# Taking the tensor work of the mixing stages off GpSimd: the S5 scan rebuilt for VectorE, the weight splits, rotary products and decays moved, one convolution tap given to ScalarE

## The chip, the cores and the metric

The kernel runs on one core of a Trainium2 chip. The metric is the device time of one execution in microseconds (us). The core has five engines that run their own instruction queues in order: TensorE for matmuls (PE in the profile; PEld are its weight loads), VectorE (DVE), ScalarE (ACT), GpSimd (POOL) and SyncE (SP), which here only starts DMA transfers.

## The reference

The reference is a two-layer trunk over 256 context tokens and 256 latent tokens of width 1024, all in float32. Each layer has a mixing stage and a mixture-of-experts stage (MoE). The mixing stage, cut to what matters:

```
u, z, xbc, dtr, q, k, v, gates = split_cols(h @ w_in)
ya = s5_branch(u, ...)          # complex diagonal SSM: B u, scan, C h, gelu, glu
yb = ssd_branch(z, xbc, dtr...) # 5-tap convolution, silu, chunked scan, gated norm
yc = attention_branch(q, k, v)  # rotary, 128-token window plus context
out = (sum_k sigmoid(gates_k) * (y_k @ w_branch_k)) @ w_out
```

The S5 branch has 32 groups of 16 channels, 64 complex states each, in two directions:

```
bur = einsum('gpk,bngk->bngp', bbr, u);  bui = ...
h_n = a * h_(n-1) + bu_n          # complex, per group and state; reversed for direction 1
y   = einsum('gkp,bngp->bngk', c_re, hr) - einsum('gkp,bngp->bngk', c_im, hi)
```

Layer 0 needs outputs for context and latent tokens (512), layer 1 for the latent tokens alone (256). The MoE stage reads 16 experts' weights, three matrices of 4 MB each.

## The kernel before, in words

**Order.** The program is written layer by layer as `mixing(l)` and `moe(l)`. A list scheduler with a timing model of its own fixes each engine's order when the kernel is built, so instructions of branches that do not depend on each other are interleaved. Tiles wait by semaphores on what was in their space before.

**Weights and splits.** Float32 products of good accuracy are made from split halves. `load_w` (L103) lets SP load a 128x1024 block of weights into `w` (three buffers), ACT copies it rounded into `wh` (L110), and a subtraction makes the rest, `wl` (L113). Two buffers each hold `wh` and `wl`. The subtraction goes to POOL and DVE in turn (`turn`, `wcnt`). `mm3` (L122, L125) then multiplies `wh` by both halves of the activations and `wl` by the high half.

**S5.** `s5_gen` (L585) handles four groups of channels and both directions in one block, eight blocks in a layer, in one set of buffers (four `rb` tiles) and one PSUM bank (`bank("s5")`, one buffer). The names that the steps touch:

- `bc`, `Ub`: the block's parameters and inputs, loaded from the ACT queue (L610, L611). `bb` (L614 to L619) is the discretised B, its real half on DVE and its imaginary half on POOL.
- `gp` (L631 to L633) are the powers that bring eight steps of B together, `cp9` (L637 to L639) those of C. `tmp` holds the second products. Direction 0 is made by DVE (`e = V`), direction 1 by POOL. `ti` are `gp`'s transposes (L642, L643).
- `pk` (L648), `kr` (L650 to L653) and `kd` are the short convolution kernels: `kr` lies in the last 240 columns of `tmp`, goes to DRAM (`kd`, L655) and comes back as `W` (L657).
- `er`, `ei` (L665 to L667) are rotations, the first on DVE, the second on POOL. `px` (L674) are the inputs of the scan; they are rotated (L683 to L688; the two sums on POOL), scanned (L691, eight scans of 64 steps with a decay from `rho`), rotated back (L696 to L699, half on POOL) and written into `hs` (L706 to L709, half on POOL).
- `yp` (L713, L715) is the output, L719 to L722 its gelu, L723 the store to DRAM (`ad`).

**Others on POOL.** The splits of the branch outputs (`splits`, L736; L1122; L1130), one product of the state decay (L898), two of the rotary (L924, L925), the gate product (L958), half of the query splits (L992), the router's weights (L1144, L1145), and preparations that the change leaves alone: memsets, powers in `s5_params` and the one-hot scaling in the MoE stage (L1272).

**Convolution.** `ev_x` (L791) copies a PSUM tile into `xp` (ACT, L800), makes five taps on DVE (L809 and four times L812), a tanh on ACT (L814) and a last product on DVE (L816), for eight tiles in a layer.

**End of a mixing stage.** Three calls of `merge` (L1077) multiply the branch outputs and add them up in `acc` (L1094 to L1097). The first two need the SSD and the attention branch, the third needs S5's outputs through a glu (L1116 to L1122). `w_out` and the router (L1140 to L1200) follow, and then the MoE stage, whose weights stream through the buffers that the mixing stage held.

Of the kernel before, what the change touches and what calls it, by code (L numbers as in the profile page):

```python
# [66 lines left out]
def tile_trunk(ctx: ExitStack, tc: tile.TileContext, a, out, dbg=None, stop=None):  # L67
# [220 lines left out]
    def s5_params(l, sl):  # L288
# [113 lines left out]
        Aa = keep("aa", 640).rearrange("p (q i) -> p q i", i=10)  # L402
        Ab = keep("ab", 640).rearrange("p (q i) -> p q i", i=10)
        G.memset(Aa, 0.0)
        G.memset(Ab, 0.0)
        for dst, lo_, hi_, sgn in ((Aa, PR, PI, 1.0), (Ab, PI, PR, -1.0)):
            for d in range(2):
                for h, (src, sg) in enumerate(((lo_, sgn), (hi_, 1.0))):
# [3 lines left out]
                    ov = ov[:, :, :, 1:10] if d == 0 else ov[:, :, :, 0:9]  # L412
# [50 lines left out]
    def mixing(l, mods):  # L463
# [121 lines left out]
        def s5_gen():  # L585
# [11 lines left out]
            xr, xi = sl(4, 64), sl(4, 64)  # L597
# [3 lines left out]
            kr = tmp.rearrange("p a b -> p (a b)")[:, 784:1024]  # L601
            pq = ti.rearrange("p a b -> p (a b)").rearrange("p (i t c) -> p i t c", i=4, t=4)
            G.memset(bst, 0.0)  # L603
            G.memset(hs, 0.0)
            kd = dram.tile([8, 4, 32, 240], F32, name="kd%d" % l)

            for b in range(8):
# [4 lines left out]
                frb, fib = (sp[n][:, g8, None].to_broadcast([128, 8, 16]) for n in ("fr", "fi"))  # L612
                t0, t1 = (tmp[:, 4 * i].rearrange("p (t k) -> p t k", k=16) for i in range(2))
                V.tensor_tensor(bb[:, 0], bc[:, 0], frb, op=OP.mult)  # L614
                V.tensor_tensor(t0, bc[:, 1], fib, op=OP.mult)
                V.tensor_tensor(bb[:, 0], bb[:, 0], t0, op=OP.subtract)
                G.tensor_tensor(bb[:, 1], bc[:, 0], fib, op=OP.mult)
                G.tensor_tensor(t1, bc[:, 1], frb, op=OP.mult)
                G.tensor_tensor(bb[:, 1], bb[:, 1], t1, op=OP.add)  # L619
                S.activation(bst[0:64, :, 0:16], bb[0:64, 0], AF.Copy)  # L620
                S.activation(bst[64:128, :, 0:16], bb[64:128, 1], AF.Copy, scale=-1.0)
                for d in range(2):
                    e = V if d == 0 else G
                    td = slice(4 * d, 4 * d + 4)
                    cp = cp9[:, td, 1 - d:9 - d, :]
                    S.activation(cp9[:, td, 8 * d, :], bc[:, 4, td], AF.Copy)
                    A_, B_ = (sp[n][:, 8 * b + 4 * d:8 * b + 4 * d + 4] for n in ("Aa", "Ab"))
                    sh = [128, 4, 16, 8]
                    tg = tmp[:, td].rearrange("p t (k s) -> p t k s", s=8)
                    gv = gp[:, td].rearrange("p t (k s) -> p t k s", s=8)  # L630
# [3 lines left out]
                    sh = [128, 4, 8, 16]  # L634
                    tc_ = tmp[:, td].rearrange("p t (i k) -> p t i k", k=16)
                    iw = slice(2 - 2 * d, 10 - 2 * d)
                    e.tensor_tensor(cp, bc[:, 2, td, None, :].to_broadcast(sh), A_[:, :, iw, None].to_broadcast(sh), op=OP.mult)  # L637
                    e.tensor_tensor(tc_, bc[:, 3, td, None, :].to_broadcast(sh), B_[:, :, iw, None].to_broadcast(sh), op=OP.mult)
                    e.tensor_tensor(cp, cp, tc_, op=OP.add)  # L639
# [3 lines left out]
                    S.activation(ti[:, td].rearrange("p t n -> p (t n)"), pt, AF.Copy)  # L643
# [920 lines left out]
```

## Time and profile before

| | |
|---|---|
| time, median of 3 runs | 2175.32 us (2174.04 to 2178.39) |
| profiled execution, first to last instruction | 2175.6 us; the profile gives no other time of its own |
| instructions | 29618 |
| busy: PE, DVE, POOL, ACT | 1879.4, 1040.2, 589.0, 554.9 us |
| mixing stages, roughly | 0 to 690 us and 1200 to 1680 us |
| MoE stages, roughly | 690 to 1200 us and 1680 to 2175 us |

The profile shows one execution. "Busy" is the time in which an engine worked on an instruction; what an engine waits for is inferred from semaphores. The ends of matmuls are modelled, so that a busy PE may still have waited a little within that time. The time of the profiled execution lies 0.3 us above the median of the runs.

### The profile page before, as it was taken

The page shows a single profiled execution, that of the slowest core. Times are in us where ns is not written, and L with a number is a line of the kernel's source. Part 1 is how long each engine was busy: PE and PEld are TensorE (multiplying, and loading weights), DVE is VectorE, ACT ScalarE, POOL GpSimd, SP SyncE. Part 2 cuts the span into 40 slices and gives each one's busy share as a digit, 9 for nine tenths or more (in the row PEclk, how much of TensorE's full clock was granted, in tenths as well). Part 3 has the DMA queues.
Part 4 walks back from the last instruction along what each step waited for, and adds up shares of the span by engine and source line. Part 5 has one row for each costly group of instructions (what it writes and reads, how often), then busy time and mean ns, then how long its engine had stood idle before and what let it go on. Part 6 is the DMA issues. An engine that isn't in the chain of part 4 may idle for free. (4 is left out here: it accounts for less than half of the span.)

```text
span 2175.6 us, 29618 instructions
## 1 busy us (share of the span) xinstructions
PE 1879.4 (86%) x11292; PEld 1127.1 (52%) x11292; DVE 1040.2 (48%) x2234; ACT 554.9 (26%) x1200; POOL 589.0 (27%) x644
## 2 busy tenths in 40 slices
PE   6899999999999997986897898989998997776675
PEld 4577777788787432322332576778897322111111
DVE  6888786663256227121123469788656222212122
ACT  4335644442343100000000433535443100000000
POOL 1645476542242002000003235486533000000000
PEclk9999989999998998998898998989998899999798
DMA  9464333336345998999999355343477899999997
GB/s 268 156 183 127 114 90 107 99 104 220 90 155 203 410 349 351 409 408 409 404 409 351 107 185 172 107 129 86 125 244 271 348 409 409 409 409 409 409 409 274
DMA packets 265310, 561.72 MB, mean 258 GB/s; under 512 B 44048, under 2 KB 132560, under 8 KB 264912
## 3 DMA queue, kind: packets, MB, share of 16 engines
q1 hardware_dynamic: 232864, 541.83, 68.0%
q10 hardware_dynamic: 32304, 18.00, 3.0%
q8 instruction: 89, 1.46, 0.3%
q14 instruction: 53, 0.43, 0.1%
HBM read 552.00 MB, written 7.77 MB: 257 GB/s over the span
## 5 line engine op out<-in xcount | busy, mean ns | idle before, releaser
L122 PE MATMUL bk_mm<-hh,wh 128*128 128x512 f32 (+1 forms) x704 | 254.2, 375 | 12.5 <-ACT xp L800 6.7
L122 PE MATMUL bk_mm<-hl,wh 128*128 128x512 f32 (+1 forms) x704 | 247.6, 365 | 0.0
L113 POOL TENSOR_TENSOR wl<-w,wh 128x1024 fp32r<-128x1024 f32 x64 | 157.0, 2452 | 223.5 <-ACT wh L110 171.1
L110 ACT ACTIVATE wh<-w 128x1024 fp32r<-128x1024 f32 x140 | 147.9, 1058 | 215.9 <-PE bk_mm L122 106.6
L125 PE MATMUL bk_mm<-hh,wl 128*128 128x512 f32 (+1 forms) x704 | 163.0, 361 | 1.5 <-POOL wl L113 1.5
L122 PEld LDWEIGHTS bk_mm<-hh,wh 128*128 128x128 f32 x704 | 139.6, 199 | 36.1 <-ACT xp L800 8.2
L122 PEld LDWEIGHTS bk_mm<-hl,wh 128*128 128x128 f32 x704 | 139.6, 199 | 17.7 <-issue 1.4
L113 DVE TENSOR_TENSOR wl<-w,wh 128x1024 fp32r<-128x1024 f32 x76 | 99.8, 1315 | 72.6 <-ACT wh L110 32.4
L125 PEld LDWEIGHTS bk_mm<-hh,wl 128*128 128x128 f32 x704 | 119.6, 195 | 20.0 <-POOL wl L113 1.7
L1389 PE MATMUL bk_mm<-rb,xeT 128*64 128x512 f32 x512 | 122.1, 601 | 3.3 <-DMA rb<-w_e_up 2.0
L1419 PE MATMUL bk_mm<-xw,xeT 128*32 128x512 f32 x448 | 107.3, 628 | 16.5 <-DMA xw<-w_e_gate 11.4
L1424 DVE SCALAR_TENSOR_TENSOR hd<-fth,bk_mm 64x512 f32<-64x512 f32 x16 | 10.9, 681 | 208.4 <-ACT fth L1422 208.4
L1441 DVE SCALAR_TENSOR_TENSOR YE<-bk_mm,grow 32x512 f32<-32x512 f32 x64 | 44.0, 687 | 129.6 <-PE bk_mm L1436 115.8
L1422 ACT ACTIVATE fth<-bk_mm 64x512 f32<-64x512 f32 x16 | 9.4, 590 | 377.7 <-PE bk_mm L1419 377.7
L1389 PE MATMUL bk_mm<-xw,xeT 128*64 128x512 f32 x320 | 82.1, 613 | 13.5 <-DMA xw<-w_e_gate 13.5
L603 POOL MEMSET rb<- 128x256 f32 x2 | 1.2, 588 | 319.0 <-PE bk_mm L1389 305.0
L1393 DVE SCALAR_TENSOR_TENSOR fth<-fth,bk_mm 128x512 f32<-128x512 f32 x16 | 11.0, 687 | 157.3 <-ACT fth L1392 157.3
L1389 PEld LDWEIGHTS bk_mm<-rb,xeT 128*64 128x64 f32 x512 | 40.1, 139 | 78.6 <-issue 69.8
L1409 DVE SCALAR_TENSOR_TENSOR YE<-bk_mm,grow 32x512 f32<-32x512 f32 x64 | 44.0, 687 | 73.3 <-PE bk_mm L1405 56.5
L1419 PE MATMUL bk_mm<-rb,xeT 128*32 128x512 f32 x304 | 68.0, 603 | 8.3 <-DMA rb<-w_e_up 6.1
L1366 PE MATMUL bk_ps<-YE,Gt 128*128 128x512 f32 x128 | 61.7, 612 | 11.9 <-DVE YE L1441 9.1
L1419 PEld LDWEIGHTS bk_mm<-xw,xeT 128*32 128x32 f32 x448 | 24.1, 114 | 88.7 <-issue 55.5
(560 smaller groups left out, 3883.5 us busy)
## 6 DMA issues: line engine op xcount, KB each, us to landing
xw<-w_e_gate SPq DMA_DIRECT2D x67, 1024.0 KB, 11.5
rb<-w_e_up SPq DMA_DIRECT2D x59, 1024.0 KB, 17.4
xw<-w_e_down SPq DMA_DIRECT2D x54, 1024.0 KB, 14.0
w<-w_in SPq DMA_DIRECT2D x92, 512.0 KB, 4.7
rb<-w_e_gate SPq DMA_DIRECT2D x43, 1024.0 KB, 16.6
w<-w_mod SPq DMA_DIRECT2D x80, 512.0 KB, 4.1
xw<-w_e_up SPq DMA_DIRECT2D x29, 1024.0 KB, 14.0
w<-w_e_down SPq DMA_DIRECT2D x46, 512.0 KB, 14.0
```

The costliest lines, as they stand in the source:

```text
L110: S.activation(r(hi), raw, AF.Copy)
L113: e.tensor_tensor(r(lo), raw, hi, op=OP.subtract)
L122: PE.matmul(ps, wh(m, k), xv, start=first and k == 0 and i == 0, stop=False)
L125: PE.matmul(ps, wl(m, k), xs[k](m)[0], start=False, stop=last and k == n - 1)
L1366: PE.matmul(ps, Gt[:, tt - tts[0], e // ne, :], YE[:, tt // 2 if full else 0, n, :], start=True, stop=True)
L1389: PE.matmul(ps[64 * n:64 * n + 64, :], xeT[:, k, e, :], w[:, n * 512:n * 512 + 512], start=k == 0, stop=k == 7)
L1393: V.scalar_tensor_tensor(th, th, 1.0, pg, op0=OP.add, op1=OP.mult)
L1409: V.scalar_tensor_tensor(YE[q0:q0 + 32, si, n, :], py[o:o + 32, :], 0.5, g2[o:o + 32, si, n * 512:n * 512 + 512], op0=OP.mult, op1=OP.mult)
L1419: PE.matmul(pg[o:o + 32, :], xeT[:, k, e, :], w[:, n * 512:n * 512 + 512], start=k == 0, stop=k == 7)
L1422: S.activation(th[:64], pg[:64], AF.Tanh, scale=0.5)
L1424: V.scalar_tensor_tensor(hd[64:128], th[:64], 1.0, pg[:64], op0=OP.add, op1=OP.mult)
L1441: V.scalar_tensor_tensor(YE[q0:q0 + 32, 0, n, :], py[o:o + 32, :], 0.5, g2[o:o + 32, 1, n * 512:n * 512 + 512], op0=OP.mult, op1=OP.mult)
```

## The change

The same values are computed. In `load_w`, `norm_rows`, `splits`, the glu, the query splits, the state decay, rotary, gate product, `acc` splits and router weights, `G` becomes `V`, and the alternation of `turn` goes. The first convolution tap becomes an ACT instruction with a per-channel scale and bias.

In S5, all tensor operations of POOL go to DVE, and many are joined: `bb` becomes four operations over both parts; `gp` is made of four products and one sum over both directions; `cp9` gets all nine powers at once (so ACT's copies into it, L626, go); `px` is stored with its real half in front, so that each rotation is a 512-wide product `PQ`; direction 1 is mirrored by TensorE's reading of `Ub` and of `hs` instead of by DVE; one 512-step scan takes the place of eight, with a decay tile `rho` that ACT fills in each block and whose zeros part the eight sequences; the sums that undo the rotation write both parts into `hs` in four operations. The order in the text changes too: `px` and the scan now stand ahead of `pk` and `kr`. The intermediate `xx` lies in the first half of `gp`, and `PQ` in `ti`. The tables `Aa` and `Ab` lose a column.

```diff
         S.activation(r(hi), raw, AF.Copy)
-        wcnt[0] += 1
-        e = G if turn[0][wcnt[0] % len(turn[0])] == "G" else V
-        e.tensor_tensor(r(lo), raw, hi, op=OP.subtract)
+        V.tensor_tensor(r(lo), raw, hi, op=OP.subtract)
...
+                for ri in range(2):
+                    S.activation(rho[:, 4 * ri:4 * ri + 4, 1:64], sp["rho"][:, q4, None].to_broadcast([128, 4, 63]), AF.Copy)
...
-                    e = V if d == 0 else G
-                    S.activation(cp9[:, td, 8 * d, :], bc[:, 4, td], AF.Copy)
-                    e.tensor_tensor(gv, bb[:, 0, td, :, None].to_broadcast(sh), A_[:, :, None, 1:9].to_broadcast(sh), op=OP.mult)
-                    e.tensor_tensor(tg, bb[:, 1, td, :, None].to_broadcast(sh), B_[:, :, None, 1:9].to_broadcast(sh), op=OP.mult)
-                    e.tensor_tensor(gv, gv, tg, op=OP.add)
+                    for dst, r_, tb in ((gp, 0, A_), (tmp, 1, B_)):
+                        V.tensor_tensor(dst[:, td].rearrange("p t (k s) -> p t k s", s=8),
+                                        bb[:, r_, td, :, None].to_broadcast(sh),
+                                        tb[:, td, None, d:d + 8].to_broadcast(sh), op=OP.mult)
+                V.tensor_tensor(flat(gp), flat(gp), flat(tmp), op=OP.add)
...
+                        uv = Ub[:, j, :] if d == 0 else mir(Ub[:, j, :])
...
+                for i in range(2):
+                    V.tensor_tensor(PQ[:, i], px.rearrange("p (r t) -> p r t", r=2), turn_[i], op=OP.mult)
+                V.tensor_tensor(xx[:, 0], PQ[:, 0, 0], PQ[:, 1, 1], op=OP.add)
+                V.tensor_tensor(xx[:, 1], PQ[:, 1, 0], PQ[:, 0, 1], op=OP.subtract)
+                V.tensor_tensor_scan(flat(gp)[:, :512], flat(rho), flat(gp)[:, :512], 0.0, OP.mult, OP.add)
...
+                V.tensor_tensor(cp9, bc[:, 2, :, None, :].to_broadcast([128, 8, 9, 16]),
+                                A_[:, :, :, None].to_broadcast([128, 8, 9, 16]), op=OP.mult)
+                for d in range(2):
+                    cv = ct[:, :576].rearrange("p (t i k) -> p t i k", i=9, k=16)
+                    V.tensor_tensor(cv, bc[:, 3, td, None, :].to_broadcast(sh), B_[:, td, :, None].to_broadcast(sh), op=OP.mult)
+                    V.tensor_tensor(cp9[:, td], cp9[:, td], cv, op=OP.add)
                 pk = bank("s5")
...
-                G.tensor_tensor(xr, xr, xt[:, 0], op=OP.add)
-                G.tensor_tensor(xi, xi, xt[:, 1], op=OP.subtract)
-                for t_ in range(4):
-                    for v in (xr, xi):
-                        V.tensor_tensor_scan(v[:, t_, :], sp["rho"][:, 4 * b + t_:4 * b + t_ + 1].to_broadcast([128, 64]),
-                                             v[:, t_, :], 0.0, OP.mult, OP.add)
...
+                    V.tensor_tensor(ov[0:64], pv[:, 0, 0, :, :, w_], pv[:, 1, 1, :, :, w_], op=OP.add)
+                    V.tensor_tensor(ov[64:128], pv[:, 0, 1, :, :, w_], pv[:, 1, 0, :, :, w_], op=OP.subtract)
...
-                G.tensor_tensor(r(l_[:, m, lo:]), src[:, m, lo:], h_[:, m, lo:], op=OP.subtract)
+                V.tensor_tensor(r(l_[:, m, lo:]), src[:, m, lo:], h_[:, m, lo:], op=OP.subtract)
...
-                e.tensor_scalar(yh[:, s0:], xp[:, s0:, 0:256], wc(0), hcw[:, 80 + l * 8 + i:80 + l * 8 + i + 1],
-                                op0=OP.mult, op1=OP.add)
+                S.activation(yh[:, s0:], xp[:, s0:, 0:256], AF.Identity, scale=wc(0),
+                             bias=hcw[:, 80 + l * 8 + i:80 + l * 8 + i + 1])
...
-            G.tensor_tensor(qs, qs, K("cos"), op=OP.mult)
-            G.tensor_tensor(dst, qs, m, op=OP.add)
+            V.tensor_tensor(qs, qs, K("cos"), op=OP.mult)
+            V.tensor_tensor(dst, qs, m, op=OP.add)
```

The scheduler's order at two places. The first is POOL's queue of before near the end of S5 in layer 1. In these names `rb_9571` holds `gp` and `ti`, `rb_9572` holds `tmp` and `kr`, `rb_9573` holds `cp9`, and `rb_9574` the rotations and the scan's values. L632, L633 and L638 belong to block 8; L687 to L709 belong to block 7.

```order
L113 TENSOR_TENSOR wl<-w,wh 128x1024
L632 TENSOR_TENSOR rb_9572<-rb_9572,sp_ab 128x512
L633 TENSOR_TENSOR rb_9571<-rb_9571,rb_9572 128x512
L638 TENSOR_TENSOR rb_9572<-rb_9573,sp_ab 128x512
L736 TENSOR_TENSOR yl<-qT,yh 128x256 x2
L687 TENSOR_TENSOR rb_9574<-rb_9574 128x256
L688 TENSOR_TENSOR rb_9574<-rb_9574 128x256
L736 TENSOR_TENSOR yl<-qT,yh 128x256
L697 TENSOR_TENSOR rb_9571<-rb_9574 128x4x33
L699 TENSOR_TENSOR rb_9571<-rb_9574 128x4x33
L706 TENSOR_TENSOR rb_9574<-rb_9571 64x2x32
```

This is DVE's queue of the changed kernel at the same block 7, with that kernel's line numbers: L676 and L677 finish `kr`, L697 and L698 write `hs`, L625 makes the products for block 8 (the one with `sp_ab` writes into `tmp`, where `kr` lies), L628 sums them, L109 is the weight split, L1004 and L1085 belong to attention and `merge`. Here `rb_9352` holds `gp`, `rb_9353` holds `tmp`, and `rb_9355` the rotations and `hs`.

```order
L676 TENSOR_TENSOR rb_9353<-rb_9353,bk_s_11358 128x16
L698 TENSOR_TENSOR rb_9355<-rb_9352 64x2x2x32 x2
L697 TENSOR_TENSOR rb_9355<-rb_9352 64x2x2x32 x2
L677 SCALAR_TENSOR_TENSOR rb_9353<-kc,cl,rb_9353 128x16
L625 TENSOR_TENSOR rb_9352<-rb_9353,sp_aa 128x512
L650 TENSOR_TENSOR rb_9355<-sp_e8i,sp_f8r 128x256
L109 TENSOR_TENSOR wl<-w,wh 128x1024
L1004 TENSOR_REDUCE mx<-bk_ps 128x1
L625 TENSOR_TENSOR rb_9353<-rb_9353,sp_ab 128x512
L1004 TENSOR_REDUCE mx<-bk_ps 128x1
L1085 SCALAR_TENSOR_TENSOR acc_11593<-sg,bk_mm 128x256
L628 TENSOR_TENSOR rb_9352<-rb_9352,rb_9353 128x1024
```

Block 7's own steps now stand ahead of the write into `tmp`, and that write stands in DVE's queue instead of POOL's.

The second place is DVE's queue in the convolution of layer 0, before: four taps of one tile with S5's scans and back rotation behind them.

```order
L812 SCALAR_TENSOR_TENSOR yh<-xp,cl,yh 128x512 x3
L691 SCALAR_TENSOR_TENSOR rb_1609<-sp_rho,rb_1609 128x64 x8
L696 TENSOR_TENSOR rb_1606<-rb_1609 128x256
L698 SCALAR_TENSOR_TENSOR rb_1606<-rb_1609 128x256
L816 SCALAR_TENSOR_TENSOR BC<-cth,yh 128x512
L809 TENSOR_SCALAR yh<-xp,cl 128x512
```

In the changed kernel the taps (L803) alternate with S5's sums (L656, L657), its one scan (L658), a weight split (L109) and the back rotation (L688).

```order
L803 SCALAR_TENSOR_TENSOR yh<-xp,cl,yh 128x512
L656 TENSOR_TENSOR rb_1604<-rb_1604 128x256
L657 TENSOR_TENSOR rb_1604<-rb_1604 128x256
L803 SCALAR_TENSOR_TENSOR yh<-xp,cl,yh 128x512
L658 SCALAR_TENSOR_TENSOR rb_1604<-rb_1607,rb_1604 128x512
L109 TENSOR_TENSOR wl<-w,wh 128x1024
L803 SCALAR_TENSOR_TENSOR yh<-xp,cl,yh 128x512
L688 TENSOR_TENSOR rb_1604<-rb_1604,rb_1607 128x512 x2
```

The first tap (L809) is gone from DVE's queue, and the split has come into it between two taps.

## Rows read from the trace of the kernel before

**Rows 1.** The page's head and its line of busy times.
```profile
span 2175.6 us, 29618 instructions
PE 1879.4 (86%) x11292; PEld 1127.1 (52%) x11292; DVE 1040.2 (48%) x2234; ACT 554.9 (26%) x1200; POOL 589.0 (27%) x644
```

**Rows 2.** Busy us by stretch: PE, PEld, DVE, ACT, POOL; then PEclk, DMA share, GB/s.
```profile
50.00:200.00 150.00, 133.10 (x1065) 98.54 (x1064) 129.13 (x292) 61.62 (x145) 80.95 (x114) 0.94 0.50 157
200.00:500.00 300.00, 295.01 (x2168) 229.81 (x2167) 211.12 (x461) 140.02 (x343) 164.50 (x171) 0.98 0.38 111
500.00:690.00 190.00, 186.16 (x826) 149.23 (x825) 86.22 (x142) 65.26 (x94) 65.08 (x38) 0.97 0.51 167
1250.00:1500.00 250.00, 222.93 (x1935) 181.21 (x1928) 200.60 (x395) 103.06 (x249) 132.39 (x147) 0.92 0.47 140
1500.00:1600.00 100.00, 94.05 (x768) 87.38 (x769) 67.12 (x159) 40.51 (x83) 50.81 (x56) 0.95 0.54 156
```

**Rows 3.** The same columns for instructions on `rb` tiles alone (S5's buffers).
```profile
200.00:500.00 300.00, 46.01 (x497) 37.77 (x496) 97.23 (x235) 19.89 (x58) 98.11 (x124) 0.98 0.38 111
1250.00:1500.00 250.00, 37.80 (x432) 32.24 (x432) 82.78 (x190) 15.47 (x50) 81.11 (x98) 0.92 0.47 140
```

**Rows 4.** DVE's busy us of L691 alone (eight scans a block), same stretches.
```profile
200.00:500.00 300.00, 14.57 (x48) 0.98 0.38 111
1250.00:1500.00 250.00, 18.29 (x40) 0.92 0.47 140
```

**Rows 5.** DVE's groups by form: count, busy us, mean ns; idle before.
```profile
L812 DVE SCALAR_TENSOR_TENSOR yh<-xp,cl,yh 128x512 f32<-128x512 f32 x56 | 54.7, 977 | 1.7
L1097 DVE SCALAR_TENSOR_TENSOR acc<-sg,acc 128x512 f32<-128x512 f32 x16 | 20.7, 1291 | 0.5
L1096 DVE SCALAR_TENSOR_TENSOR sg<-sg,bk_mm 128x512 f32<-128x512 f32 x16 | 11.0, 686 | 45.0 <-PE bk_mm L125 42.8 <-PE bk_mm L198 2.2
```

**Rows 6.** L113, the split: its instructions, ns least/median/most.
```profile
L113 DVE TENSOR_TENSOR wl<-w,wh x76: 1209/1224/2161, 35.7 to 1658.9; 128x1024 fp32r<-128x1024 f32 x76
L113 POOL TENSOR_TENSOR wl<-w,wh x64: 2347/2397/2854, 34.2 to 1656.4; 128x1024 fp32r<-128x1024 f32 x64
```

**Rows 7.** The chain that ended last, parts of 1522 to 1680 us: start, us, what.
```profile
1522.74 1.13 DVE wl L113
...
1527.26 0.60 DVE rb L633
...
1533.93 5.30 DMA kd<-rb
...
1539.39 1.14 POOL rb L632
...
1540.60 1.27 POOL rb L633
...
1541.95 1.06 POOL rb L638
1543.01 2.44 POOL yl L736 x2
1545.46 0.71 POOL rb L687
...
1548.14 0.62 DVE rb L691 x3
...
1549.61 1.79 POOL rb L699
...
1602.25 2.36 POOL wl L113
...
1679.76 0.69 DVE cum L455
```

**Rows 8.** Waits of the whole span: who for whom, us, times, longest.
```profile
POOL rb L632 <- DMA kd<-rb: 39.8, 8, 8.1
ACT cth L814 <- DVE yh L812: 52.2, 11, 10.5
```

More of the change, by code (lines that the diff above doesn't have):

```diff
@@ L528, in norm_rows @@
                 V.tensor_copy(r(hh[:, k, :]), h)
-                (G if k % 2 and not full else V).tensor_tensor(r(hl[:, k, :]), h, hh[:, k, :], op=OP.subtract)
+                V.tensor_tensor(r(hl[:, k, :]), h, hh[:, k, :], op=OP.subtract)
         def hv(k, t0, t1):
@@ L596, in s5_gen @@
             er, ei = sl(4, 64), sl(4, 64)
-            xr, xi = sl(4, 64), sl(4, 64)
+            rho = sl(8, 64)
             xt = sl(2, 4, 64)
@@ L611, in s5_gen @@
                 dma5(Ub, ud[4 * b:4 * b + 4].rearrange("g r c -> r g c"))
[L612 to L617, printed above, removed]
@@ L642, in s5_gen @@
                         PE.transpose(pt[:, j * 128:j * 128 + 128], gp[:, 4 * d + j], ident)
-                    S.activation(ti[:, td].rearrange("p t n -> p (t n)"), pt, AF.Copy)
+                    S.activation(ti[:, 4 * d:4 * d + 4].rearrange("p t n -> p (t n)"), pt, AF.Copy)
+                px = bank("s5")
+                pxv = px.rearrange("p (r t c) -> p r t c", r=2, t=4)
+                for d in range(2):
+                    for j in range(4):
+                        g2 = j % 2
+                        uv = Ub[:, j, :] if d == 0 else mir(Ub[:, j, :])
+                        for ri in range(2):
+                            o = pxv[64 * g2:64 * g2 + 64, ri, 2 * d + j // 2, :]
+                            PE.matmul(o if d == 0 else o.rearrange("p (s c) -> p s c", s=2),
+                                      ti[:, 4 * d + j, 64 * ri:64 * ri + 64], uv, start=True, stop=True)
@@ new lines, in s5_gen @@
+                sh = [128, 4, 9, 16]
+                ct = flat(tmp)
+                V.tensor_tensor(cp9, bc[:, 2, :, None, :].to_broadcast([128, 8, 9, 16]),
+                                A_[:, :, :, None].to_broadcast([128, 8, 9, 16]), op=OP.mult)
+                for d in range(2):
+                    td = slice(4 * d, 4 * d + 4)
+                    cv = ct[:, :576].rearrange("p (t i k) -> p t i k", i=9, k=16)
+                    V.tensor_tensor(cv, bc[:, 3, td, None, :].to_broadcast(sh), B_[:, td, :, None].to_broadcast(sh), op=OP.mult)
+                    V.tensor_tensor(cp9[:, td], cp9[:, td], cv, op=OP.add)
@@ L695, in s5_gen @@
[L695 to L709 removed]
+                w_ = slice(0 if full else 31, 63)
@@ new lines, in s5_gen @@
+                x4 = xx.rearrange("p r (t c) -> p r t c", c=64)
+                P4 = PQ.rearrange("p i r (t c) -> p i r t c", c=64)
+                if full:
+                    for i in range(2):
+                        V.tensor_tensor(PQ[:, i], xx, turn_[i], op=OP.mult)
+                else:
+                    for i, v in enumerate((er, ei)):
+                        for ri in range(2):
+                            V.tensor_tensor(P4[:, i, ri, :, w_], x4[:, ri, :, w_], v[:, :, w_], op=OP.mult)
@@ L710, in s5_gen @@
+                for g2 in range(2):
+                    ir = slice(64 * g2, 64 * g2 + 64)
+                    pv = P4[ir].rearrange("p i r (d q) c -> p i r d q c", d=2)
+                    ov = hs.rearrange("p (q g) d c -> p g d q c", g=2)[:, g2][:, :, :, w_.start + 1:64]
+                    V.tensor_tensor(ov[0:64], pv[:, 0, 0, :, :, w_], pv[:, 1, 1, :, :, w_], op=OP.add)
+                    V.tensor_tensor(ov[64:128], pv[:, 0, 1, :, :, w_], pv[:, 1, 0, :, :, w_], op=OP.subtract)
                 yp = bank("s5")
@@ L1099, in mixing @@
         acc = [m8("acc0"), m8("acc1")]
-        turn[0] = "VG" if full else "VGV"
         merge(1, y2s, 1.0, True)
```

112 lines of the change are left out of this document (37 added, 75 removed).

## Prediction

> **What bounds the kernel now.** I read the page's head first. No engine is full over the span: PE 86%, DVE 48%, POOL 27% [rows 1]. That is an average over stages with different limits, so the next view is the table of busy times by stretch [rows 2]. The change touches the mixing stages alone. In layer 0 from 200 to 690 us PE is busy for 295.0 of 300 and 186.2 of 190 us: PE bounds it and there are only 8.8 us to win. Two stretches are different. From 50 to 200 us (convolution, first S5 blocks) PE is idle for 16.9 us while DVE is 86% busy. From 1250 to 1500 us (layer 1's convolution, SSD and S5) PE is idle for 27.1 us with DVE at 80%. The granted clock is lower there too, 0.94 and 0.92 against 0.98 from 200 to 500. From 1500 to 1600 PE is idle for 6.0. Idle PE time in these rows sums to 58.8 us.
>
> Then I looked at whether POOL, where the work now sits, is dear. The same split takes a median of 1.224 us on DVE and 2.397 on POOL [rows 6]. And POOL is not free for DVE: the group at L1097, both inputs in SBUF, takes 1291 ns on average, and the group at L1096 of the same size with one input in PSUM takes 686 [rows 5]. DVE stands still in the first for nearly half its time, and I take that for time behind POOL, since groups that read PSUM keep their price beside the same POOL. The Trainium skill ("SBUF — State Buffer", Who interferes with whom) has the rule: a DVE instruction with two SBUF inputs contends with a GpSimd instruction that reads SBUF, and the loser blocks for the whole instruction. By that rule the 605 ns are time behind POOL and vanish with it; the rows agree that PSUM readers are spared.
>
> Last, the chain of waits near the end of layer 1's S5 [rows 7]. After a DMA of 5.30 us (`kd`) it runs through POOL: L632, L633, L638, L736, L687, later L699, and a split at L113. The order of POOL's queue explains it: L632 of block 8 overwrites `kr` in `tmp` and must wait for `kd` to read it, and block 7's own sums (L687) stand behind it. This wait occurs 8 times, 39.8 us in all [rows 8].
>
> **The change part by part.** *Price of DVE work with no POOL beside it.* On the chain, back to back, 512 columns cost 0.60 us (L633) and 1024 cost 1.13 (L113) [rows 7], so about 0.07 us for each instruction plus 1.035 ns a column. Scans are slower: three of 64 columns in 0.62 us, one of 256 in 0.69 [rows 7], so 2.5 ns a column, and 1.33 us for the new one of 512.
>
> *S5 on DVE.* A block of before has 32 instructions with 6808 columns besides its eight scans: 32 x 0.07 + 7.05 + 8 x 0.207 = 10.9 us. A block of after in layer 0 has 34 with 12944 columns and one scan: 2.4 + 13.4 + 1.3 = 17.1; in layer 1, with half the outputs, 15.9. But DVE did not do a block in 10.9 us. From 200 to 500 us it was busy for 97.23 us on S5's buffers [rows 3] in 48/8 = 6 blocks [rows 4], so 16.2 a block; from 1250 to 1500, 82.78 in 5 blocks, 16.6. The 5.5 us between are time behind POOL. So DVE's S5 time changes by +0.9 a block in layer 0 and -0.7 in layer 1: nothing. POOL's 98.1 and 81.1 us in these stretches go away for no price on DVE.
>
> *Other work moved to DVE.* 64 splits of 1.13 us are 72 us. The smaller ones (L736, L1130, L1122, L958, L898, L924, L925, L992, half of L529's, the router's) are about 45 of 512 and 45 of 256 columns: 45 x 0.60 + 45 x 0.33 = 42. The taps given to ACT take off 16 x 0.6 = 10. Against these 104 us stands the waiting that ends outside S5: L812, 56 x (0.977 - 0.686) = 16, and L1097, 16 x 0.605 = 10 [rows 5]. So DVE gets 78 us more if only these two groups gain, and nothing more if every group with two SBUF inputs gains as L1097 does. I take the middle, 40 us over two stages in which these rows show DVE busy for 694 of 990 us. A third of the splits lies where PE is full and DVE at 45%. DVE does not become the bound on average.
>
> *ACT* gets 16 taps and 32 fills of `rho`, and loses 32 copies: some 15 us. It is busy for at most 47% of any of these stretches [rows 2], so I cost that at nothing; if ACT were late, `wh` would be late next.
>
> *What the chain gains.* In the tail of S5 in layer 1, L632, L633 and L638 (3.5 us) no longer precede block 7's work, since the order of after has block 7's L697 and L698 ahead of the write into `tmp`. The other POOL pieces, 2.44 + 0.71 + 1.79 + 2.36 = 7.3, halve. That is 7 us; bounds 0, if DVE is busy with other things just then, and 12, with the `kd` wait. From 1250 to 1500 there are five blocks with the same pattern. Against the gain stands that `pk` now follows `px`, so that `kd` and the load of `W` have less to hide under (back rotation and `hs`, about 2.7 us, and the scan). I take 2 us a block, 10; bounds 0 and the stretch's PE idle, 27. From 50 to 200: DVE's waiting shrinks most here but the start of layer 0 also waits for weights; 6 of PE's 16.9 idle, bounds 0 and 17. From 200 to 690: 2, bounds 0 and 9. Splits and the router after 1600: 2. The lower clock in the two loose stretches costs PE about 0.08 x 250 + 0.06 x 150 = 29 us; I count 3 of them, bounds 0 and 29, because it is only worth what PE's idle time gives.
>
> *What it costs.* The wait for `kd` moves from POOL's queue into DVE's. Between the end of `kr` (L677) and the write into `tmp` stand four instructions, 0.60 + 0.33 + 1.13 + about 0.5 = 2.6 us; `kd` took 5.30. So DVE can stand still for 2.7 us in a block, 43 us in 16, with everything of the attention, `merge` and the splits queued behind. Where DVE has room that is free; in the tight stretches (7 blocks) it is 19 us, of which I charge 4. Bounds: 0, and 25 for the case below.
>
> Sum: -7 - 10 - 6 - 2 - 2 - 3 + 4 = -26. The profiled execution ran 2175.6 us, 0.3 above the median of the runs; 2175.3 - 26 = **2149**. The MoE stages move with their start, not in length: their weights flow as before.
>
> **Rivals.**
> *Slower: DVE's queue is the new bottleneck.* The place is 1250 to 1500 us and the conv stretch of layer 0, the mechanism the `kd` wait at the head of DVE's queue. For it: DVE at 200.6 of 250 plus five full waits of 5.30 plus some 10 of moved work is 237, or 95%. An in-order queue that full delays PE. It decides from about 90%. Price: some 12 us in each tight stretch, less the chain's gain of few: 2175 + 20 = 2195. Against it: the order has 2.6 us of cover and S5's DVE time does not grow. The Trainium skill ("Perfetto Trace Analysis", Optimizing Scalar/DVE Operations) speaks for this side: with DVE saturated, moving work to ScalarE or even GpSimd may make sense; it adds that between DVE and GpSimd this might not help. By its first half the change goes the wrong way and would end near 2195; the 1291 against 686 ns [rows 5] speak for the second.
> *No change.* PE is what it is at 98% from 200 to 690; if layer 1's idle PE time is due to ACT, DMA and the dependences of attention, halved POOL steps only lengthen waits elsewhere. For it: the chain has DMA pieces of 5 us. Then 2171 to 2179.
> *A larger gain.* If POOL was behind most of the idle time, the 55 us of PE idle in the stretches (58.8 less 3.8 of the merges) close by two thirds and half the clock's 29 us return: 2175 - 37 - 15 = 2123, down to 2100. For it: DVE's taps at 977 ns hold ACT back for 52.2 us [rows 8], and through it `wh`.
>
> **How the numbers follow.** Chances: the forecast 0.50 (own range 2130 to 2166), the larger gain 0.20, no change 0.12, slower 0.18. About 0.2% (4.4 us) is what a measurement of this kernel can tell from no change. So faster 0.70, same 0.12, slower 0.18. The range leaves out the worst of the slower case and the best of the larger gain, about a tenth each: 2105 to 2190.
>
> **What would show it.** POOL below 80 us busy, with memsets, powers and one-hots alone. L1097 at 0.69 us, L812 near 0.75, splits at 1.22. DVE busy between 1040 and 1100. S5's DVE time about 16 to 17 us a block. PE idle between 1250 and 1500 falling to about 15 us of a shorter stretch. Waits of DVE at L625 for `kd` of a few us, some 8 to 16 times: if they reach 5 us each, the slower case holds. The forecast is wrong if DVE is over 90% busy in layer 1's stretch, or if PE's idle time stays where it was under other names.

## The result, and the profile after

The changed kernel takes **2193.02 us** (median of 5 runs, 2188.84 to 2197.7) against 2178.39 of the kernel before beside it: ratio 1.0081, 95% interval 1.0056 to 1.0105. It is slower by 0.8%, where 2149 was forecast with a range of 2105 to 2190. The profiled execution has a span of 2187.0 us, 11.4 more than before, at a mean granted clock of 0.931 (before 0.933).

The page's line of busy times answers to [rows 1]:

```profile
PE 1879.1 (86%) x11292; PEld 1128.9 (52%) x11292; DVE 1066.0 (49%) x2328; ACT 570.8 (26%) x1216; POOL 53.5 (2%) x148
```

POOL fell from 589.0 to 53.5 us and DVE rose by 25.8: the work moved as the diff says, and PE's busy time is what it was. DVE's groups by form (columns as in [rows 5, 6]):

```profile
L109 DVE TENSOR_TENSOR wl<-w,wh 128x1024 fp32r<-128x1024 f32 x140 | 171.0, 1222 | 110.8 <-ACT wh L108 78.3 <-PE bk_mm L121 28.2 <-ACT sg L1075 1.8
L803 DVE SCALAR_TENSOR_TENSOR yh<-xp,cl,yh 128x512 f32<-128x512 f32 x56 | 41.7, 745 | 0.9 <-ACT yh L800 0.7
L1087 DVE SCALAR_TENSOR_TENSOR sg<-sg,bk_mm 128x512 f32<-128x512 f32 x16 | 11.0, 688 | 20.3 <-PE bk_mm L121 20.3
L1088 DVE SCALAR_TENSOR_TENSOR acc<-sg,acc 128x512 f32<-128x512 f32 x16 | 11.0, 688 | 0.3
```

The group with two inputs in SBUF, 1291 ns before, costs 688 now, as much as its neighbour that reads PSUM. All 140 splits take 1222 ns. The prices were right. Next, busy times by stretch, as in [rows 2]:

```profile
50.00:200.00 150.00, 136.12 (x1120) 100.71 (x1119) 130.16 (x320) 71.47 (x161) 18.14 (x54) 0.95 0.52 159
200.00:500.00 300.00, 284.62 (x2089) 223.38 (x2088) 208.79 (x436) 137.71 (x334) 0.55 (x4) 0.96 0.40 118
500.00:690.00 190.00, 185.31 (x830) 147.86 (x828) 101.29 (x167) 64.99 (x94) 0.37 (x2) 0.99 0.45 140
1250.00:1500.00 250.00, 221.29 (x1919) 179.77 (x1918) 193.32 (x413) 106.95 (x250) 0.94 (x14) 0.89 0.47 143
1500.00:1600.00 100.00, 93.01 (x774) 86.21 (x772) 72.74 (x162) 44.90 (x96) 0.00 (x0) 0.93 0.52 154
```

PE's idle time fell from 16.9 to 13.9 us in the first stretch, but rose from 5.0 to 15.4 in the second and from 27.1 to 28.7 in layer 1's stretch, where it was to fall to about 15. DVE there is at 77%, not above 90. The waits have new names:

```profile
PE bk_s L702 <- DMA rb<-kd: 21.9, 8, 8.1
ACT cth L805 <- DVE yh L803: 20.1, 6, 5.8
```

POOL's 39.8 us for `kd` [rows 8] are gone. In their place PE waits 21.9 us in 8 waits for the load of `W`; before, PE's own waits for it were 2.0 us. The longest, in layer 1's fifth block, on PE's timeline (start, duration, instruction; in brackets the idle time before it and what ended it):

```profile
1461.06 0.67 PE L672 MATMUL bk_s<-rb,rb 128*32 128x128 f32 x16
1469.82 0.61 PE L702 MATMUL bk_s<-rb,rb 128*128 128x32 f32 x2 [8.09 <-DMA rb<-kd]
...
1474.93 0.77 PE L964 MATMUL bk_ps<-dgr,kc 128*128 128x128 f32 x2
```

In these 8.09 us `pk` is copied, corrected, written to DRAM and read back as `W`. Behind the product with `W` stands L964, the gated norm's diagonal, which was late for a reason of its own. DVE's timeline of the same time:

```profile
1457.56 0.17 DVE L958 TENSOR_REDUCE zv<-zss 128x2 f32<-128x8 f32 x1
...
1461.13 1.22 DVE L658 TENSOR_TENSOR_SCAN rb<-rb,rb 128x512 f32<-128x512 f32 x1
1462.27 0.13 DVE L212 TENSOR_TENSOR rs_u<-rs_y 128x2 f32<-128x2 f32 x1
1462.32 1.22 DVE L109 TENSOR_TENSOR wl<-w,wh 128x1024 fp32r<-128x1024 f32 x1
...
1463.94 0.15 DVE L213 SCALAR_TENSOR_TENSOR rs_u<-rs_u,rs_v 128x2 f32<-128x2 f32 x1
...
1471.01 0.48 DVE L963 TENSOR_SCALAR dgr<-kc,rs_y 128x128 f32<-128x128 f32 x2
```

From the row sum to the diagonal is a chain of 13 short dependent instructions of some 0.15 us. Between most of them a scan, splits or S5 products of 0.4 to 1.2 us have slipped in: 13.45 us from start to start, against 7.03 before:

```profile
1452.51 0.15 DVE L967 TENSOR_REDUCE zv<-zss 128x2 f32<-128x8 f32 x1
...
1459.55 0.47 DVE L972 TENSOR_SCALAR dgr<-kc,rs_y 128x128 f32<-128x128 f32 x2
```

In layer 0 the loss is at two other places. The larger one is from 240 to 300 us, after:

```profile
240.00:300.00 60.00, 49.92 (x434) 38.46 (x432) 46.78 (x90) 33.39 (x90) 0.00 (x0) 0.92 0.39 113
```

and before:

```profile
240.00:300.00 60.00, 58.88 (x504) 44.59 (x503) 50.87 (x103) 34.69 (x91) 39.80 (x44) 1.00 0.39 116
```

PE is busy for 9.0 us less. Its named waits from 250 to 300 us are for ScalarE's `cpart` (3.4 us), for what stands ahead of `gp`'s transposes (L632, 3.0 us), for `mcol` (1.6 us) and for `W` (1.4 us). The other place is the end of the attention. PE from 490 us:

```profile
490.30 1.05 PE L1024 MATMUL bk_ps<-kc,pr 128*128 128x128 f32 x8
491.65 2.00 PE L1028 MATMUL bk_ps<-vt,pT 128*128 128x64 f32 x16 [0.31 <-ACT pT L1026]
494.77 0.66 PE L1041 MATMUL bk_ps<-kc,yt 128*128 128x128 f32 x4 [1.11 <-DVE yt L1038]
496.77 1.22 PE L118 MATMUL bk_mm<-yh,wh 128*128 128x512 f32 x2 [1.35 <-ACT yh L726]
```

PE has nothing else to do between these than the attention's own chain. The last S5 block ended at 456.9 us (before 490.5). Busy times of 480 to 520 us, after:

```profile
480.00:520.00 40.00, 35.90 (x173) 28.09 (x173) 18.62 (x38) 13.56 (x29) 0.00 (x0) 0.91 0.43 120
```

and of the kernel before, where S5's products and merge windows fill it:

```profile
480.00:520.00 40.00, 40.00 (x210) 34.19 (x210) 15.58 (x30) 12.53 (x19) 12.21 (x15) 1.00 0.82 263
```

### The profile page after: what moved, and what is told of

The parts are those of the page before. It is cut to its first block, busy times and chain, and to the rows that moved or that the text cites. A ratio compares the mean times of both kernels' runs of the same rounds, so it can differ in the third digit from the quotient of the medians.

```text
span 2187.0 us, 29006 instructions
## 1 busy us (share of the span) xinstructions
PE 1879.1 (86%) x11292; PEld 1128.9 (52%) x11292; DVE 1066.0 (49%) x2328; ACT 570.8 (26%) x1216; POOL 53.5 (2%) x148
## 4 chain that ended last, share of the span: by engine, by line
PE 53%; DMA 25%; DVE 6%; ACT 2%; issue 1%; POOL 1%; SPq 0%; ACTq 0%; DVEq 0%; POOLq 0%
PE bk_mm L118 12%; PE bk_mm L1378 7%; PE bk_mm L121 5%; PE bk_mm L1408 4%; PE bk_mm L1394 4%; DMA rb<-w_e_up 3%; DMA wl<-w_e_up 3%; DMA wh<-w_e_up 3%; PE bk_ps L1272 3%; DMA xw<-w_e_gate 2%; DMA w<-w_e_up 2%; DMA xw<-w_e_down 2%; PE bk_mm L1425 2%; DMA w<-w_e_gate 2%; PE bk_ps L1028 1%; PE bk_ps L1355 1%
## 5 line engine op out<-in xcount | busy, mean ns | idle before, releaser
L109 DVE TENSOR_TENSOR wl<-w,wh 128x1024 fp32r<-128x1024 f32 x140 | 171.0, 1222 | 110.8 <-ACT wh L108 78.3
L161 PE MATMUL bk_mm<-w,sil 128*32 128x128 f32 x1280 | 58.1, 288 | 14.2 <-DMA w<-w_mod 13.8
L1381 ACT ACTIVATE fth<-bk_mm 128x512 f32<-128x512 f32 x16 | 9.6, 597 | 216.8 <-PE bk_mm L1378 216.8
```

Of the source, the lines that this page charges most:

```text
L109: V.tensor_tensor(r(lo), raw, hi, op=OP.subtract)
L161: PE.matmul(ps[32 * j:32 * j + 32, :128], sil[:, 2 * u + i, :], w[:, i, j * 128:j * 128 + 128], start=u == 0 and i == 0, stop=u == 3 and i ...
```

## The experiments

Every ratio is to the kernel before, timed beside the run on the same chip; its median there lay between 2173.86 and 2178.39 us, so that ratios compare better than times. S5's parts are called by the names in the code.

**Four theories.** W: the round trip of `W` is exposed, since `pk` now follows `px` and the scan. D: VectorE's queue is too full. N: the norm's short chain is held up in it. F: S5's steps are missing as filler in layer 0. Against all of them stands C: the list scheduler makes another order of every text, and the time goes with the order, not with the work (the first expectations call it L).

**1. `W` without the round trip**

```diff
-dma5(W[:, j, :], bass.AP(tensor=kd.tensor, ...))
+dma5(W[:, j, :], a["s5bc"][:, l, b, j * 128:j * 128 + 128])
```

> The changed kernel, but W is loaded from the constant array of S5 (same four transfers, same sizes) and no longer from what the block has just written, so the S5 kernel matrix in the output is another one. Theory W (TensorE stands at the W product of yp for a round trip through DRAM that now begins after px and the scan): the 21.9 us of TensorE's waits for kd at L702 are gone, and the time falls below the kernel before, to 2165 to 2178. Rival D (the loss is VectorE's: the 104 us of moved work and the S5 block stand in one queue): the waits at L702 turn into waits for VectorE, 2187 to 2196. Rival L (the scheduler's new order as such costs the time): anywhere, but not tied to L702; 2185 to 2195.

2202.63 us, ratio 1.0124 (1.0102 to 1.0146). The waits for `kd` are gone, and the kernel is no faster. The total does not decide it: against the changed kernel 8 us are lost ahead of layer 0's first window matmul and 13 in layer 0, where only 3.6 us of these waits had been. Layer 1 had 18.2 us of them. It takes 416.8 us (421.6 with the round trip; bounds of this stage below), and PE's idle time in it is 37.4 us (37.0): other waits stand in their place. From 1200 to 1700 us:

```profile
PE bk_mm L118 <- ACT wh L108: 8.0, 2, 6.7
PE bk_s L632 <- DVE rb L712: 7.9, 2, 4.6
```

The norm's chain took 16.21 us here. From the product with `W`, ahead of which the 8.09 us had stood, to the diagonal PE now waits 2.5 us for `hs`, 4.8 for the gelu and the transposes behind it, and 0.9 for the diagonal, 8.2 in all. Theory W falls as the one cause: `W` was the last of several things that come late together. (Two controls below point the same way: runs 11 and 15 both have 8.9 us of PE's waits for `kd` in layer 1, half of the changed kernel's, and take 410.6 and 422.2 us for it.)

**2. The S5 kernel ahead of `px`**

```diff
+cp9 ..., pk, kr, dma5(kd), dma5(W)
 px = bank("s5")
 ... px, rotation, scan ...
-cp9 ..., pk, kr, dma5(kd), dma5(W)
```

> The changed kernel with cp9, pk, kr and the two transfers put back ahead of px and the scan in the text, where the kernel before has them. Theory W: kd has the whole scan to hide under, TensorE's waits for kd at the W product fall to 2 to 5 us, and the time is 2168 to 2182, a little above the run without the round trip because px and the scan start later by the 3.8 us of cp9. Rival D: no change, 2187 to 2197. Rival L: another order, another time, with the waits for kd not deciding it.

2178.51, ratio 1.0008 (0.9992 to 1.0024), and PE's waits for `kd` fall to 4.1 us: both as theory W expects. Layer 1 takes 404.5 us with 25.0 us of idle PE time (421.6 and 37.0 after, 419.3 and 33.9 before), but layer 0 takes 651.5 (644.1, 636.4). Whether layer 1's 17 us come from the round trip or from the order is tested by run 10.

**3. `yp` behind the step's other work**

```diff
+yield
 yp = bank("s5")
 ...
 dma5(ad[...], ab_)
-yield
```

> The changed kernel with one line moved: the generator gives way before yp instead of behind the store, so that yp and gelu of a block stand in the text where the next block begins, behind the other work of a step. Theory W: no wait of TensorE for kd is left, nor for hs, and ScalarE no longer stands at gelu; 2158 to 2175. Rival D: the same DVE work, 2183 to 2195. Rival L: as theory W on the waits, but with a time that does not follow them.

2191.37, ratio 1.0068 (1.0042 to 1.0093). In 15 of the 16 blocks the scheduler puts `yp` within 145 places of where it was among TensorE's 11292 matmuls, and PE's waits for `kd` are still 18.9 us in 9. The edit did not do what it was for and decides nothing about W.

**4, 5. The parts alone**

```diff
# 4: only the hunks of s5_params and s5_gen
# 5: all other hunks (splits, rotary, decays, conv tap)
```

> The kernel before with the rebuilt S5 alone; splits, rotary, decays and the conv tap stay where they were, so GpSimd keeps some 250 us of work. Theory W: the order that exposes the round trip is in it, so TensorE waits for kd at the W product by 15 to 25 us and the time stays near the changed kernel, 2184 to 2198. Rival D: VectorE is freed of 104 us of moved work, 2165 to 2178. Rival L: anywhere.

> The kernel before with all of the change except S5: splits, rotary, decays go to VectorE and a conv tap to ScalarE; S5 keeps its text and its GpSimd work. If the parts add up, this is 2192 less 2202 of the S5 run, so about 8 to 10 us under the kernel before: 2164 to 2172. Rival D (moved work overloads VectorE): 2183 to 2195. Theory F (what costs time is where S5's steps stand in the order, as filler for TensorE): S5's last gelu of layer 0 stays near 490 us, layer 0 keeps its 636 us within 4, and the time is 2165 to 2180.

S5 alone 2201.61 (1.0119, 1.0093 to 1.0145), the rest alone 2189.69 (1.0057, 1.0038 to 1.0076), both together 1.0081. Apart they cost 1.2% and 0.6%, together 0.8%: they do not add up. D expected S5 alone to be fast (2165 to 2178) and additivity the rest; both fail. D's 2183 to 2195 for the rest alone did come, and F's 2165 to 2180 did not. W expected waits for `kd` of 15 to 25 us with S5 alone; they are 8.9. Against D as a cost of DVE's work stands run 11: the same work on DVE, 20 us less time.

**6, 7. The Newton steps on GpSimd**, in the changed kernel and in that of run 2

```diff
-V.tensor_tensor(t, y, y, op=OP.mult) ...
+G.tensor_tensor(t, y, y, op=OP.mult) ...   # gated norm only, 14 instructions
```

> The changed kernel with the three Newton steps of the gated norm's reciprocal root (128x2 and 128x4 values, 14 small instructions) on the idle GpSimd instead of VectorE. Theory N: in layer 1 the 13.45 us from the row sum (L958) to the first diagonal (L963) are mostly S5 and split instructions of 0.4 to 1.2 us that slip between the dependent small ones in VectorE's in-order queue; with the chain away from them it takes 5 to 9 us, the diagonal comes 4 to 8 us earlier, and TensorE's gap of 8.1 us there shrinks by as much: 2180 to 2189. Theory W (the gap is the load of W, which ended it): the gap stays 8 us under the name of kd, 2190 to 2196.

> The run with the S5 kernel ahead of px (2178.5), with the Newton steps on GpSimd too. Theory N: the chain of layer 1 falls from 9.2 to 5 to 8 us and the time to 2170 to 2176. Theory W: nothing left to win there, 2176 to 2181.

The chain gets shorter, as N says. Run 6, timeline:

```profile
1466.44 0.16 DVE L967 TENSOR_REDUCE zv<-zss 128x2 f32<-128x8 f32 x1
...
1469.51 1.20 POOL L212 TENSOR_SCALAR rs_v<-rs_v 128x2 f32<-128x2 f32 x1 [110.29 <-DVE rs_t L207]
...
1474.66 0.23 POOL L218 TENSOR_SCALAR rs_y<-rs_y 128x2 f32<-128x2 f32 x1
1474.92 0.48 DVE L972 TENSOR_SCALAR dgr<-kc,rs_y 128x128 f32<-128x128 f32 x2 [3.53 <-POOL rs_y L218]
```

8.48 us in place of 13.45, and PE's wait for `kd` at this place is 5.18 us in place of 8.09. But the time is 2188.95 (1.0065, 1.004 to 1.0091), at the edge of N's range and with an interval that overlaps the changed kernel's, and in run 7 2179.52 (1.0011, 0.9992 to 1.003) beside 2178.51 without it, outside N's 2170 to 2176. That the chain set the end of the kernel is not shown. The Trainium skill ("Perfetto Trace Analysis", Optimizing Scalar/DVE Operations) says that where DVE is not saturated but makes bubbles elsewhere, breaking up instructions may let work end sooner. The 13.45 us behind 1.2 us instructions are such a case; no run here broke those up.

**8 to 10. Two S5 steps of layer 0 later**, in the changed kernel, in that of before, and together with run 2

```diff
-SS = [[(0, 1), (0, 3), (1, 1), (1, 3)], [(0, 1), (0, 3), (1, 1), (1, 3)]]
+SS = [[(0, 3), (1, 3)], [(0, 1), (0, 3), (1, 1), (1, 3)]]
```

> The changed kernel with two of layer 0's eight S5 steps taken out of the SSD loop, so that the last two blocks stand behind the attention in the text, as filler for TensorE. Theory F: in layer 0 S5 ended 37 us earlier than before (gelu of the last block at 454 instead of 491 us), so nothing was left to put between the last heads of the attention, where TensorE stood 4 us and its clock fell; with two blocks there, that stretch (480 to 520 us) has under 1.5 us of idle time and a granted clock of 1.0, and layer 0 gives back 5 to 9 us: 2183 to 2188. Rival D: the order of S5 is not the matter, 2190 to 2196.

> The kernel before with two of layer 0's eight S5 steps taken out of the SSD loop, the edit that gave the changed kernel 22 us. Theory S (in the changed kernel a step is all VectorE's, and in the SSD loop of layer 0 it stands in front of the short instructions that TensorE waits for; with half of it on GpSimd it did so less): the kernel before gains less than 8 us, 2169 to 2178. Theory C or a gain of the placing as such, whatever the engine: 10 to 22 us, 2155 to 2167.

> The changed kernel with both edits: the S5 kernel ahead of px (15 us gained, in layer 1) and two steps of layer 0 later (22 us gained, most in layer 0). If both are mechanisms of their own, in different layers, they add up: 2152 to 2160, faster than both kernels. Theory C (each was a lucky order): they don't add, 2165 to 2180.

Run 8: 2171.01, ratio 0.9974 (0.9958 to 0.9989), 22 us below the changed kernel and the only version of all that is measurably faster than the kernel before. Layer 0 takes 634.7 us, 9.4 less than in the changed kernel, where F said 5 to 9. But F's reason does not hold: S5 now ends at 484.0 us, and the stretch at the end of the attention still has 2.6 us of idle time and a granted clock of 0.91 (after 4.1 and 0.91). Between 260 and 360 us PE is busy for 94.1 us at a clock of 0.98 (after 90.2 at 0.91). The same edit makes the kernel before slower, 2185.95 (1.005, 1.0032 to 1.0068), and the two edits that each gained 15 and 22 us give 2184.32 together (1.0042, 1.0026 to 1.0059), above C's range too. In run 10 layer 1 takes 417.3 us with 36.2 us of idle PE time. Its text for layer 1 is that of run 2, and PE's waits for `kd` there are 3.0 us; so run 2's 404.5 us do not follow from the hidden round trip alone. S, F and addition all fail. So the question became how much any exchange moves.

**11 to 18. Controls: the same work in another text**, each in the changed kernel and in the kernel before

```diff
# 11, 12: ei ahead of er (two independent groups)
-for ... in enumerate(((er, ...), (ei, ...))):
+for ... in enumerate(((ei, ...), (er, ...))):
# 13, 14: the loads of a block
-dma5(bc, ...); dma5(Ub, ...)
+dma5(Ub, ...); dma5(bc, ...)
# 15, 16: direction 1 ahead of direction 0 (gp and transposes; in the kernel before cp9 too)
-for d in range(2):
+for d in (1, 0):
# 17, 18: the group of er and ei moved up, ahead of the transposes / ahead of pk
```

> A control. The changed kernel with two independent groups of three VectorE instructions in another order in the text (ei before er). The work is the same; only what the scheduler makes of it changes. Theory C (the 0.8 per cent is what any other order gives or takes): the time moves by 5 us or more against 2193. If the loss is one of the mechanisms named so far, it stays within 4 us: 2189 to 2197.

> The same control for the kernel before: ei ahead of er in the text. Theory C: moves by 5 us or more against 2177. Else 2173 to 2181.

> Second control on the changed kernel: the two loads of a block (bc and Ub) change places in the text, the work is the same. Theory C (the time is mostly what the scheduler's order makes of it; the orders of this kernel scatter by 10 us or more): any time between 2165 and 2200, and likelier below 2193 than above, since 2193 is the highest of those measured with the whole change in but for none. Theory M (the change has a cost of its own of 0.8 per cent, and the control that gave 2173 was a lucky one): 2188 to 2200.

> The same exchange of the two loads in the kernel before. Theory C: the scatter is there too, 2168 to 2195, likelier above 2177. Theory M: 2172 to 2182, as the first control.

> Third control on the changed kernel: direction 1 ahead of direction 0 in the products of gp and in the transposes, the work is the same. Theory C: 2165 to 2200, likelier below 2193. Theory M: 2188 to 2200.

> The same for the kernel before: direction 1 ahead of direction 0 in gp, cp9 and the transposes. Theory C: 2168 to 2195, likelier above 2177. Theory M: 2172 to 2182.

> Fourth control on the changed kernel: the group of er and ei stands ahead of the transposes in the text and no longer behind px; few instructions change places (395 lines of difference in TensorE's order). The three controls so far gave 0.9989, 1.0087 and 1.0078 of the kernel before, the changed kernel itself 1.0081. Theory C: between 0.997 and 1.010. Theory M: 1.006 to 1.010.

> Fourth control on the kernel before: the group of er and ei ahead of pk (148 lines of difference in TensorE's order). The three so far gave 1.0018, 1.0029 and 1.0082. Theory C: between 0.998 and 1.009, so that the means of the two kernels' five orders lie within 0.5 per cent of each other. Theory M: 0.998 to 1.003.

Medians, ratios, and from each profiled execution the length of four stages: layer 0 from its first window matmul to the router's ranking, the MoE stage up to layer 1's first window matmul, layer 1 to its last window matmul, and the rest; and PE's idle time in the two mixing stages. The profiled execution can lie off its median: that of "after, loads" took 2181.38 us, 10.8 below.

| order | us | ratio (95%) | layer 0 | MoE 0 | layer 1 | rest | idle 0 / 1 |
|---|---|---|---|---|---|---|---|
| before | 2178.39 | 1 | 636.4 | 552.7 | 419.3 | 533.1 | 22.3 / 33.9 |
| before, ei first | 2179.58 | 1.0018 (1.0002-1.0033) | 636.5 | 556.2 | 420.1 | 532.1 | 22.0 / 30.9 |
| before, loads | 2182.08 | 1.0029 (1.0015-1.0042) | 635.1 | 554.0 | 425.6 | 532.6 | 24.9 / 38.7 |
| before, direction | 2191.85 | 1.0082 (1.0064-1.0101) | 651.6 | 552.6 | 420.4 | 533.0 | 35.1 / 38.6 |
| before, turns | 2173.19 | 0.9997 (0.9982-1.0011) | 633.4 | 555.0 | 413.4 | 532.8 | 23.4 / 31.6 |
| after | 2193.02 | 1.0081 (1.0056-1.0105) | 644.1 | 554.5 | 421.6 | 533.5 | 30.6 / 37.0 |
| after, ei first | 2172.97 | 0.9989 (0.9973-1.0005) | 640.7 | 550.3 | 410.6 | 532.6 | 28.8 / 29.8 |
| after, loads | 2192.22 | 1.0087 (1.0063-1.011) | 643.2 | 551.9 | 418.4 | 532.9 | 33.0 / 33.6 |
| after, direction | 2192.15 | 1.0078 (1.0062-1.0094) | 641.0 | 555.9 | 422.2 | 532.8 | 28.6 / 32.1 |
| after, turns | 2191.35 | 1.0077 (1.0057-1.0098) | 648.7 | 555.9 | 421.1 | 531.1 | 34.1 / 36.3 |

Work-preserving edits move the kernel before by up to 0.8% and the changed one by 0.9%: the two groups overlap. Not every control favours C. Run 11 moved as C said and run 16 left M's range, but run 12 moved less than C's 5 us, run 14 sits at M's edge, and the others fit both. The means are 1.0025 and 1.0062. Their difference is 0.37%, with an interval from the scatter of the two fives of -0.18 to +0.93% (five orders chosen by hand are no random sample). So theory M, a cost of the change of its own of 0.8%, is not shown, though four of the five changed orders lie within 0.1% of each other; and a gain of 26 us (1.2%) is excluded for these orders. Runs 2, 3, 8 and 10 of the changed kernel and run 9 of the kernel before are other texts of the same work too, though chosen in the hope of a gain. With them the changed orders reach from 0.9974 to 1.0087, and the means differ by 0.16%.

Where the means differ is layer 0, 643.5 against 638.6 us, with 31.0 against 25.5 us of idle PE time; layer 1 is the same, 418.8 and 419.7, with 33.8 and 34.7 idle. The 5.0 us of layer 0 have an interval of -3 to +13, so this loss is not clear of the scatter either; the profiled executions differ by 3.2 us in the mean, the medians by some 8. From 480 to 520 us all five changed orders leave PE idle for 3.4 to 5.4 us and S5 has ended by 434 to 461. Of the five of before, four have none there and S5 ends at 487 to 491. The fifth is the slow one:

```profile
480.00:520.00 40.00, 34.93 (x182) 27.74 (x182) 18.44 (x36) 12.71 (x25) 11.28 (x15) 0.91 0.66 204
```

Its S5 ended at 492.1. So in these ten that stretch goes with the time of layer 0, but it does not set it: run 8 has 2.6 us of idle time there and a layer 0 of 634.7 us.

## Why the prediction was wrong

**The prices held.** POOL under 80 us, splits at 1.22, L1097 at 0.69 and L812 at 0.745 (0.75 said), DVE at 1066 (1040 to 1100 said), all as written. S5's DVE time, 93.4 and 92.2 us in the stretches with 5 and 6 scans, is 18.7 and 15.4 us a block, where 16 to 17 was said and the borders cut blocks. The Trainium skill ("SBUF — State Buffer", Who interferes with whom) gave the same forecast for L1097, and 688 ns agrees with it. ACT's wait for the taps fell from 52.2 to 20.1 us. The charge of 4 us for DVE's wait for `kd` was about right: DVE waited 3.2 us in 2 waits.

**The step that failed** is the one headed "What the chain gains": the 7 us of the tail and the 10 us "2 us a block" of layer 1 took POOL's pieces on one chain for the length of the stage. With them gone the next arrival was hardly sooner: `W`, the norm's diagonal, `wh`, the weights of `w_mod`. Over five orders each, layer 1 gained 1 us (419.7 less 418.8, interval -6 to +8) and PE's idle time there 1, where 17 had been counted, and 3 more for the clock. In the kernel timed PE's idle time from 1500 to 1600 us, where the tail lies, went from 6.0 to 7.0 us, and the granted clock from 1250 to 1500 us from 0.92 to 0.89. The trace of before had a hint: of PE's own named waits in layer 1, 1200 to 1680 us, only 2.4 us are directly for POOL. The largest (us, times, longest):

```profile
PE bk_mm L125 <- POOL wl L113: 1.5, 2, 0.8
```

The term set against the gain, that `kd` and `W` have less to hide under, got no number of its own; it became PE's 18.2 us of waits for `W` in layer 1 (before 0.6). The sentence set down for "No change", that shorter POOL steps only lengthen waits elsewhere, describes the result, and the prediction's own sign of being wrong came true: PE's idle time from 1250 to 1500 us is 28.7 us (before 27.1) under other names. Run 1 shows it on one spot: the wait for `W` is taken away, and 8.2 us of other waits stand where its 8.09 were.

**A bound was missing.** For 200 to 690 us the sum had 2 us of gain, bounds 0 and 9. Nothing excluded a loss, and the kernel timed has one of 7.7 us over layer 0 (5.0 in the mean of five orders, which the scatter leaves open). That PE had been 98% busy there can be read as the scheduler's success in laying S5 between other work, which a new S5 can undo. Of the 6 us for 50 to 200, PE's idle time gave 3.0; the matmuls of L161 ran 4 to 9 us ahead of those of before at 240 us and 1.8 behind at 284.

**The slower rival had the size for a wrong reason.** It said 2195 by DVE's wait for `kd`. DVE waited 3.2 us for it, and it was busy for 77% of layer 1's stretch. What a DVE at 90% would do was set down, not measured, and no run here reaches it.

**The order was taken as given.** The range held the doubt about prices, not the 0.9% by which an exchange of two independent groups moves the changed kernel (0.2% the kernel before). The 0.2% named as what a measurement can tell is right for one build; for a question about the work it is the scatter of builds that counts. Whether the 0.8% of this one build has a single cause stays open. Run 2 gave it back where theory W looked for it, but run 10 did not keep it there; run 8 gave it back, but not at the place that F named.

## What to carry to other kernels

Where a list scheduler sets the order, first build the same work from two or three harmless rewritings and time those: their scatter, 0.8 to 1.1% here, is the least that a change must show before its mechanism is discussed. A wait's name in the profile tells who came last, not what would be won without it; ask when the second-last came. And where the critical engine is full, a change that leaves that engine's own work alone has nothing to win and can lose.

## What was not expected of the hardware

In run 1 the clock granted to TensorE was at half while the profile shows it busy for 17.5 of 20 us: 500 to 520 us, the end of layer 0's attention.

```profile
500.00:520.00 20.00, 17.54 (x68) 14.28 (x68) 4.68 (x14) 6.05 (x15) 0.00 (x0) 0.50 0.22 55
```

A 128x512 matmul took 0.77 us there and 0.39 at 523 us, when the merge's matmuls had come back:

```profile
501.01 0.77 PE L998 MATMUL bk_ps<-kvt,q__3848 128*128 128x512 f32 x1
...
522.89 0.39 PE L118 MATMUL bk_mm<-hh,wh 128*128 128x512 f32 x1
```

Ahead of the fall PE had done the attention's matmuls of 64 to 256 columns with waits between them: from 485 to 490 us it was busy for 3.9 us at the upper level of 2.4 GHz, from 490 to 495 the granted clock was 0.63, and from there to 520 it was 0.50. By estimate the 17.5 us are work for about 8.8 at the upper level, so the clock cost at most some 8.8 us here, less where PE would have waited for others instead; the visible idle time is 2.5.

On GpSimd, a 128x2 instruction of the Newton steps took 0.19 to 0.23 us (DVE 0.15), but two of them in run 6 took 1.20 and 0.68 (start, duration):

```profile
1469.37 1.23 DVE L637 TENSOR_TENSOR rb<-rb,rb 128x1024 f32<-128x1024 f32 x1
1469.51 1.20 POOL L212 TENSOR_SCALAR rs_v<-rs_v 128x2 f32<-128x2 f32 x1 [110.29 <-DVE rs_t L207]
...
1470.63 0.76 DVE L675 TENSOR_TENSOR rb<-rb,sp_ab 128x576 f32<-128x576 f32 x1
1470.76 0.68 POOL L214 TENSOR_TENSOR rs_u<-rs_y 128x2 f32<-128x2 f32 x1
```

Each ends 0.05 to 0.11 us behind a DVE instruction with two inputs in SBUF that had started before it. The rest of 110 us is not the reason: in layer 0 the same step took 0.23 us after a rest of 165. So it is not only DVE that stands behind POOL, as at L1097; POOL also stands behind DVE. Run 7 has four more such instructions, of 0.58 to 1.09 us, and each ends 0.05 to 0.10 us behind a DVE instruction of that kind.
